# A two-layer hybrid decoder trunk on one core: reordered projection groups, stepwise waits, first loads on one queue

## The chip, the cores and the metric

The kernel runs on one core of one Trainium2 chip. The metric is the device time of one execution in microseconds (us); lower is better. The kernel before took 1836.92 us in the median of three runs (1834.95 to 1837.13). The profile shows one execution in which every engine's instructions are recorded: TensorE (PE, with its weight loads as PEld), VectorE (DVE), ScalarE (ACT), GpSimd (POOL) and SyncE (SP), which issues nearly all DMA transfers.

## The reference

Sequence 512, model width 1024, two layers, all in float32. Each layer computes

```
h    = RMSNorm(x)
proj = h @ w_in                        # q_a, kv_a, g_a, q_b, k_b, v_b, uv
o_a  = sparse attention(q_a, kv_a, sigmoid(g_a))
         # 8 heads in 2 groups; per head: softmax over compressed blocks (keys and values
         # by a small gelu MLP), over selected blocks, over a window; gated sum of the three
o_b  = differential attention(q_b, k_b, v_b)
         # 4 heads: softmax(q1 k1) - lambda * softmax(q2 k2), times v, RMSNorm per head
o_c  = u * (causal W_s per 128-position chunk @ RMSNorm(gelu(v)) + b)   # SGU
x    = x + (sum over a, b, c of sigmoid(h @ w_merge + b) * (o @ w_branch)) @ w_out
h    = RMSNorm(x)
x    = x + (silu(h @ w1) * (h @ w3)) @ w2
```

and a last RMSNorm follows. Queries and keys of the attentions (but for the compressed branch) are rotated by position (RoPE). With 512 positions and 8 blocks of 64, all eligible blocks are selected, so the selected branch is a causal softmax over the whole sequence, as the window branch is.

## The kernel before

**Arithmetic.** The activations lie with channels on the partitions (tiles of 128 x 512). Each float32 operand is split into a high and a low part (`h`, `lo`), and each product is three matmuls of 512 columns (`mm3`, lines 172 to 174): high by high, low weights by high, high weights by low. Weights come in chunks of 128 x 1024 from DRAM (`wr`, 3 buffers), are split by a ScalarE copy (line 152) and a DVE or POOL subtraction (line 155) into `wh` and `wl` (3 buffers each). A chunk feeds 24 matmuls.

**Tasks and lanes.** `layer_tasks` lists the main work of a layer: tasks of dense matmuls, each with its weight chunks, taken in order by `run`. `kvc` and `u0` to `u3` are projections; `wk`, `wv` the compression MLPs; `vv` the v half of the SGU; `V` the sparse attention's values and gates; `KR`, `QA0`, `QA1`, `KB0`, `QB0`, `KB1`, `QB1` are groups of keys or queries with rotation, two chunks and 48 matmuls each; `vb` holds the values of the differential attention, four chunks; `merge_tasks` gives eight gates and eight branch products per branch; then come the output projection and the FFN. Beside the main work run two lanes (`aux_tasks`): one with the tables of sines and cosines, the compression tails (`cmpk`, `cmpv`) and the SGU, one with the attention: `nsa0`, `nsa1` (query groups of the sparse attention, each 32 units of one head, branch and 128-row block) and `diff0`, `diff1`. Every `yield` of a main task is worth its planned nanoseconds (650 for three matmuls of 512 columns), and the lanes step until they have spent as much; a lane's step is worth what it yields (W_NSA, W_DIFF or a number). A task or lane entry starts only when all in its `need` list is done; a main task that needs a lane's work makes the lanes step without main work beside them.

**Ticks.** `later(n, f)` puts f off by n ticks; a tick is one main or lane step. `ensure(key)` runs at once all that is put off under the key, `settle(key, w)` yields w until none is left. D_ROPE holds the ticks between a rotated group's evacuation and its high copy, its low part, its write to DRAM and its read back; D_OA those of the head outputs.

**Order on the engines.** The program's text gives each instruction its priority; a list scheduler of the framework then sets each engine's order from estimated durations, so an instruction can be passed by a later one that is estimated to be ready sooner. All engines and SP work their queues in order.

**Rotation.** `rope_pair` (lines 613 to 673) multiplies the two PSUM results by cosine and sine on DVE, combines them on POOL (lines 633, 634), splits on ScalarE and DVE (638, 641), writes eight pieces `rp_d` to DRAM (line 649) and reads them back with another layout (`q` in four reads, line 669; keys in eight, line 661).

**Sparse attention.** `nsa` computes per unit the logits (lines 827, 828), a row minimum on DVE (816), an exponential on ScalarE (818), the scaling with the gate on POOL (853), a transpose on TensorE (870), its split on ScalarE (871) and DVE (877), and the product with the values into the one PSUM bank `o` (891). `cmp_soft` does the compressed branch, with a mask on POOL (776). A head's result lies in two halves of 64 partitions that have to be added: ScalarE copies the lower half to SBUF (`otmp`, line 907), and a tick later DVE adds the upper half from PSUM (910), once per head.

**Buffers.** Tiles of 4 KB per partition share 36 slots (`t4`), those of 2 KB 12 slots (`t2`).

**Start.** `setup` loads the first two weight chunks on ScalarE's queue, and on SP's the parameters, x in five transfers, a third chunk, x again by rows and the constants; TensorE meanwhile runs 12 matmuls on zeros.

Of the kernel before, what the change touches and what calls it, by code (L numbers as in the profile page):

```python
# [11 lines left out]
F32 = mybir.dt.float32  # L12
# [16 lines left out]

D_FIN = (10, 17, 31, 34)  # L30
D_CMP = (0, 5, 8, 12, 15, 26)
D_ROPE = (2, 11, 16, 19)
D_MX, D_ACT, D_OA, D_XP = (25, 27), (7, 19), (1, 4, 17), 2
D_NORM = (10, 13)
W_NSA, W_DIFF, LAG = 500, 1300, 3
WARM = 12
POOLED = {"g": 512}
(P_AN, P_FN, P_BM, P_SG, P_SUB, P_PK, P_PV, P_FIN) = (0, 8, 16, 40, 44, 45, 61, 77)
# [39 lines left out]
class Kern:  # L78
# [11 lines left out]


    def t4(self, name, shape, dt=F32):
        return self.sb.tile(shape, dt, name=name, tag="t4", bufs=36)

    def t2(self, name, shape=(P, S), dt=F32):
        return self.sb.tile(list(shape), dt, name=name, tag="t2", bufs=12)

    def small(self, name, n, bufs=4):
        return self.sb.tile([P, n], F32, name=name, tag=name, bufs=bufs)
# [122 lines left out]
    def setup(self):  # L222
# [3 lines left out]
        wh = [self.sb.tile([P, 1024], F32R, name="wh", tag="wh", bufs=3) for _ in range(2)]  # L226
        wl = [self.sb.tile([P, 1024], F32R, name="wl", tag="wl", bufs=3) for _ in range(2)]
        warm = self.t2("warm", dt=BF16)
        for j in range(2):
            nc.scalar.dma_start(raw[j], A["wst"][self.index(j)[0]])  # L230
        nc.sync.dma_start(self.par[0], A["par"][0])
        for k in range(2):
            nc.sync.dma_start(self.xT[0][:, k, :], A["xT"][0, :, k, :])
        for c in range(1, 4):
            nc.sync.dma_start(self.xT[c], A["xT"][c])
        self.ones = self.const("ones", [P, 2])
        nc.gpsimd.memset(self.ones, 1.0)
        self.mhalf = self.const("mhalf", [P, 4])
# [4 lines left out]
        wp = self.bank("t")  # L243
        for _ in range(WARM):
            nc.tensor.matmul(wp, warm[:, 0:P], warm, start=True, stop=True)
        half = [slice(0, S), slice(S, 2 * S)]
        self.n_dma = 2
        tok = [self.t4("xtok", [P, 1024]) for _ in range(TT)]
        self.dma_to(2)
# [361 lines left out]
    def rope_pair(self, name, raw=None):  # L611
# [13 lines left out]
        def fb(ps):  # L625
            nc = self.nc
            t2, t3 = self.t2("t2"), self.t2("t3")
            if raw is not None:
                nc.scalar.activation(st["raw"][:, 1, :], ps, AF.Copy)
            nc.vector.tensor_tensor(t2, ps, self.sinR, op=OP.mult)  # L630
            nc.vector.tensor_tensor(t3, ps, self.cosR, op=OP.mult)
            o1, o2 = st["t1"], st["t4"]
            nc.gpsimd.tensor_tensor(o1, o1, t2, op=OP.subtract)
            nc.gpsimd.tensor_tensor(o2, o2, t3, op=OP.add)
            pcs = [self.t4("pc", [P, 2, S], F32R) for _ in range(2)]
            for p, o in zip(pcs, (o1, o2)):
                def hi(p=p, o=o):
                    nc.scalar.activation(p[:, 0, :], o, AF.Copy)

                def lo(p=p, o=o):  # L640
                    nc.vector.tensor_tensor(p[:, 1, :], o, p[:, 0, :].bitcast(F32), op=OP.subtract)
                self.later(D_ROPE[0], hi, name)
                self.later(D_ROPE[1], lo, name)

            def out():
                d = self.dr.tile([4, 32, 4, S], F32, name="rp_d", tag="rp_d", bufs=2)
                for j, p in enumerate(pcs):
                    for h in range(4):
                        nc.sync.dma_start(d[j::2, :, h, :].rearrange("a p t -> p a t"),
                                          p[32 * h:32 * h + 32].bitcast(F32))  # L650
                st["d"] = d

            def back():
                d = st["d"].rearrange("a p h t -> (a p) h t")
                if name[0] == "K":
                    kh = [self.t4("kh", [P, 2, S], F32R) for _ in range(2)]
                    kl = [self.t4("kl", [P, 2, S], F32R) for _ in range(2)]
                    for c in range(2):
                        for x, k in enumerate((kh, kl)):
                            for r in range(2):  # L660
                                nc.sync.dma_start(k[c][64 * r:64 * r + 64].bitcast(F32),
                                                  d[64 * x:64 * x + 64, 2 * c:2 * c + 2, :])
                    self.rot[name] = (kh, kl)
                else:
                    q = [self.t4("q2", [P, 2, S], F32R) for _ in range(2)]
                    for c in range(2):
                        for j in range(2):
                            h = 2 * c + j
                            nc.sync.dma_start(q[c][:, j, :].bitcast(F32), d[:, h, :])
                    self.rot[name] = q  # L670
            self.later(D_ROPE[2], out, name)
            self.later(D_ROPE[3], back, name)
# [158 lines left out]
    def nsa(self, g):  # L831
# [47 lines left out]
        def sC(u):  # L879
# [21 lines left out]
            if half == 1 and kind == 1:  # L901
                ob = OB.pop(hh).rearrange("p a t -> p (a t)")
                if hh % 2 == 0:
                    st["o"] = self.t2("oa")
                oo = st["o"]
                tmp = self.t2("otmp")
                nc.scalar.activation(tmp[0:64], ob[64:128], AF.Copy)

                def fin():
                    nc.vector.tensor_tensor(oo[64 * (hh % 2):64 * (hh % 2) + 64], ob[0:64], tmp[0:64], op=OP.add)  # L910
                self.later(D_OA[0], fin, "oa")
                if hh % 2 == 1:
                    t = self.t4("oa", [P, 2, S], F32R)
                    self.oa[2 * g + hh // 2] = t

                    def hi_():
                        nc.scalar.activation(t[:, 0, :], oo, AF.Copy)

                    def lo_():
                        nc.vector.tensor_tensor(t[:, 1, :], oo, t[:, 0, :].bitcast(F32), op=OP.subtract)  # L920
                    self.later(D_OA[1], hi_, "oa")
                    self.later(D_OA[2], lo_, "oa")
# [316 lines left out]
    def layer_tasks(self, l):  # L1239
# [85 lines left out]
        g_w("k", 3)  # L1325
        g_vv(2)
        g_vv(3)
        g_w("v", 0)
        add("V", [("v", c) for c in range(3)], g_v)
        g_w("v", 1)  # L1330
        add("KR", [("KR", "A"), ("KR", "B")], g_kr, need=["tables"])
        g_w("v", 2)
        g_w("v", 3)
        add("QA0", [("QA0", "A"), ("QA0", "B")], g_rope("QA0", 0))
        add("QA1", [("QA1", "A"), ("QA1", "B")], g_rope("QA1", 1))
        self.merge_tasks(add, l, "c", True, False, ["sgu"])
        add("vb", [("vb", c) for c in range(4)], lambda i0: self.tm(i0, self.xg, self.vb_evac, 2, 512))
        add("KB0", [("KB0", "A"), ("KB0", "B")], g_rope("KB0"), need=["nsa1"])
        add("QB0", [("QB0", "A"), ("QB0", "B")], g_rope("QB0"))
        add("KB1", [("KB1", "A"), ("KB1", "B")], g_rope("KB1"))  # L1340
        add("QB1", [("QB1", "A"), ("QB1", "B")], g_rope("QB1"))
        self.merge_tasks(add, l, "a", False, False, ["nsa1"])
# [29 lines left out]
    def aux_tasks(self, l):  # L1372
# [9 lines left out]
        Y = []  # L1382

        def nsa(g):
            if g == 0:
                yield 7000
            self.ensure("QA%d" % g)
            self.cmp_soft(g)
            yield from self.nsa(g)

        def diff(p):
            if p == 0:
                yield 7000
            self.ensure("QB%d" % p)
            yield from self.diff(p)
        Y.append(("nsa0", ["V%d" % l, "QA0%d" % l, "cmpv%d" % l], lambda: nsa(0)))
        Y.append(("nsa1", ["QA1%d" % l], lambda: nsa(1)))
# [167 lines left out]
```

## Time and profile before

| | |
|---|---|
| median of three runs | 1836.92 us (1834.95 to 1837.13) |
| the profiled execution | 1836.91 us |
| its span | 1835.1 us, 23472 instructions |
| busy: PE, PEld, DVE, ACT, POOL | 1788.1, 1490.7, 979.4, 729.4, 372.0 us |
| chain that ended last, by engine | PE 88%, DVE 5%, POOL 2%, ACT 2%, issue 2%, DMA 1% |
| DMA | 208.45 MB, 114 GB/s in the mean |

Busy time is the time in which an engine executes an instruction; matmuls are pipelined and overlap, so a busy TensorE is not TensorE at its peak. The chain that ended last is followed back from the last instruction, at each step to what released it or to the instruction before it on its engine.

### The profile page before, as it was taken

Reading aid. Unit: us, or ns where it says so; the run is one execution under the profiler, and the core shown is the slowest. Engines: PE = TensorE matmul, PEld = TensorE weight load, DVE = VectorE, ACT = ScalarE, POOL = GpSimd, SP = SyncE. Lnnn points to the kernel's source line nnn. Section 1 sums busy time; section 2 is a strip of 40 time slices with the busy share of each in tenths; the row PEclk is TensorE's granted clock in tenths of the full one; section 3 lists DMA queues with packets and bytes.
Section 4 is the critical chain, followed back from the end, with each engine's and each line's share of the span. In section 5 each row is a group of like instructions: output and inputs, shape, how many; then the busy total and the mean of one; then the engine's idle time right before and its main releaser. Section 6 shows DMA issues by size and latency. Waiting matters only on the chain.

```text
span 1835.1 us, 23472 instructions
## 1 busy us (share of the span) xinstructions
PE 1788.1 (97%) x8690; PEld 1490.7 (81%) x8690; DVE 979.4 (53%) x1931; ACT 729.4 (40%) x1303; POOL 372.0 (20%) x363
## 2 busy tenths in 40 slices
PE   9998999999999999999999899999999999999997
PEld 6886888778888888888888778887788888888887
DVE  7766774656454444433357576656555544444323
ACT  5535663345343233222334366634443432332222
POOL 0124331344330000000012343314443200000001
PEclk9999999999999999999999999999999999999999
DMA  6472112743232222223243621145422322222221
GB/s 246 154 215 90 36 64 90 217 136 133 81 115 92 96 100 92 103 93 126 106 148 112 189 81 53 58 135 171 168 101 98 109 92 95 101 92 103 92 102 59
DMA packets 71441, 208.45 MB, mean 114 GB/s; under 512 B 9376, under 2 KB 11808, under 8 KB 71328
## 3 DMA queue, kind: packets, MB, share of 16 engines
q1 hardware_dynamic: 71040, 205.91, 33.8%
q8 instruction: 69, 1.13, 0.2%
q10 hardware_dynamic: 288, 1.05, 0.2%
q14 instruction: 44, 0.36, 0.1%
HBM read 187.92 MB, written 19.01 MB: 113 GB/s over the span
## 4 chain that ended last, share of the span: by engine, by line
PE 88%; DVE 5%; POOL 2%; ACT 2%; issue 2%; DMA 1%; SPq 0%; DVEq 0%; POOLq 0%; ACTq 0%
PE ps_g L173 24%; PE ps_g L172 24%; PE ps_g L174 24%; PE ps_t L870 2%; PE ps_o L891 2%; PE ps_g L212 1%; PE ps_g L213 1%; PE ps_g L214 1%; PE ps_s L827 1%; PE ps_s L828 1%; DVE wl L155 1%; POOL mix L1072 1%; PE ps_o L988 1%; DVE e L816 1%; PE ps_o L212 1%
## 5 line engine op out<-in xcount | busy, mean ns | idle before, releaser
L152 ACT ACTIVATE wh<-wr 128x1024 fp32r<-128x1024 f32 (+2 forms) x320 | 315.6, 989 | 673.9 <-PE ps_g L174 372.9
L172 PE MATMUL ps_g<-xg,wh 128*128 128x512 f32 x1400 | 553.8, 396 | 4.0 <-DVE sm L961 1.6
L173 PE MATMUL ps_g<-xg,wl 128*128 128x512 f32 x1400 | 548.3, 392 | 2.2 <-DVE wl L155 2.2
L174 PE MATMUL ps_g<-xg,wh 128*128 128x512 f32 x1400 | 547.2, 391 | 0.0
L155 DVE TENSOR_TENSOR wl<-wr,wh 128x1024 fp32r<-128x1024 f32 (+2 forms) x308 | 359.3, 1169 | 256.2 <-ACT wh L152 255.2
L172 PEld LDWEIGHTS ps_g<-xg,wh 128*128 128x128 f32 x1400 | 263.7, 188 | 57.3 <-ACT e L818 1.9
L174 PEld LDWEIGHTS ps_g<-xg,wh 128*128 128x128 f32 x1400 | 263.7, 188 | 55.3
L173 PEld LDWEIGHTS ps_g<-xg,wl 128*128 128x128 f32 x1400 | 264.3, 189 | 53.4 <-DVE wl L155 3.3
L818 ACT ACTIVATE e<-e,nm 128x128 f32<-128x128 f32 (+1 forms) x192 | 107.1, 559 | 118.9 <-DVE nm L816 112.6
L172 PE MATMUL ps_g<-act,wh 128*128 128x512 f32 (+1 forms) x374 | 141.0, 377 | 0.0
L173 PE MATMUL ps_g<-act,wl 128*128 128x512 f32 (+1 forms) x374 | 140.8, 376 | 0.0
L174 PE MATMUL ps_g<-act,wh 128*128 128x512 f32 (+1 forms) x374 | 140.8, 376 | 0.0
L853 POOL TENSOR_SCALAR e<-e,sm,ga 128x128 f32<-128x128 f32 (+3 forms) x128 | 82.9, 650 | 144.0 <-DVE sm L852 126.2
L816 DVE CUSTOM_DVE_ANT_0 e<-ps_s,con 128x128 f32<-128x128 f32 (+1 forms) x192 | 91.5, 482 | 33.1 <-PE ps_s L828 31.3
L452 POOL TENSOR_TENSOR acc<-acc,sq 128x512 f32<-128x512 f32 x18 | 29.4, 1634 | 381.1 <-ACT sq L451 381.1
L1129 DVE TENSOR_TENSOR fb<-ps_g,R 128x512 f32<-128x512 f32 x44 | 30.4, 692 | 129.1 <-PE ps_g L174 129.1
L155 POOL TENSOR_TENSOR wl<-wr,wh 128x512 fp32r<-128x512 f32 x48 | 71.9, 1497 | 99.3 <-ACT wh L152 67.9
L1120 DVE TENSOR_TENSOR fa<-ps_g,R 128x512 f32<-128x512 f32 x44 | 30.4, 692 | 95.3 <-PE ps_g L174 95.3
L173 PEld LDWEIGHTS ps_g<-act,wl 128*128 128x128 f32 x374 | 70.4, 188 | 13.0
L172 PEld LDWEIGHTS ps_g<-act,wh 128*128 128x128 f32 x374 | 70.4, 188 | 12.8
L174 PEld LDWEIGHTS ps_g<-act,wh 128*128 128x128 f32 x374 | 70.4, 188 | 12.8
L877 DVE TENSOR_TENSOR pt<-ps_t,pt 128x128 fp32r<-128x128 f32 (+3 forms) x128 | 61.4, 487 | 22.8 <-ACT pt L871 21.2
(242 smaller groups left out, 2574.3 us busy)
## 6 DMA issues: line engine op xcount, KB each, us to landing
wr<-in_wst SPq DMA_DIRECT2D x266, 512.0 KB, 3.2
rp_d<-pc SPq DMA_DIRECT2D x112, 128.0 KB, 2.5
wr<-in_wst SPq DMA_DIRECT2D x48, 256.0 KB, 2.8
q<-rp_d SPq DMA_DIRECT2D x32, 256.0 KB, 3.9
kh<-rp_d SPq DMA_DIRECT2D x24, 256.0 KB, 6.0
kl<-rp_d SPq DMA_DIRECT2D x24, 256.0 KB, 7.1
xT<-in_xT SPq DMA_DIRECT2D x7, 512.0 KB, 6.8
xtok<-in_xtok SPq DMA_DIRECT2D x4, 512.0 KB, 9.0
```

What stands on the lines that cost most here:

```text
L152: nc.scalar.activation(h[:, :w], t[:, :w], AF.Copy)
L155: eng.tensor_tensor(lo[:, a:b], t[:, a:b], h[:, a:b].bitcast(F32), op=OP.subtract)
L172: nc.tensor.matmul(out, wh[:, c], xx[:, 0, ts], start=first, stop=False)
L173: nc.tensor.matmul(out, wl[:, c], xx[:, 0, ts], start=False, stop=False)
L174: nc.tensor.matmul(out, wh[:, c], xx[:, 1, ts], start=False, stop=last)
L212: nc.tensor.matmul(o, x[k][:, 0, ts], wh[:, sl], start=(k == 0), stop=False)
L816: nc.vector.tensor_tensor_reduce(out=e[:, :n], in0=s[:, :n], in1=self.mask[:, S - n:], scale=-0.125, scalar=3e38, op0=OP.add, op1=OP.min, ...
L818: nc.scalar.activation(e[:, :n], e[:, :n], AF.Exp, bias=nm, scale=-1.0, accum_out=sm)
L853: nc.gpsimd.tensor_scalar(e[:, :n], e[:, :n], sm, gate, op0=OP.mult, op1=OP.mult)
L870: nc.tensor.transpose(pt[:, j, :], e[:, j * P:(j + 1) * P], self.ident)
L877: nc.vector.tensor_tensor(lo, pt, hi.bitcast(F32), op=OP.subtract)
L891: nc.tensor.matmul(o[:, c0:], self.V2[kind][:, j, g, :], t[:, j, c0:], start=(kind == 0 and j == 0 and x == 0), stop=False)
```

## The change

- `setup`: ScalarE's queue loads only the parameters. SP's queue brings x and the first two weight chunks by turns, in pieces of 128 x 512 for the first four: x tile 0, first half of chunk 0, x tile 1, first half of chunk 1, x tiles 2 and 3, second half of chunk 0, x tiles 4 and 5, second half of chunk 1, x tiles 6 and 7.
- Order of main tasks: KR comes directly behind the last `vv`, QA0 between `wv1` and `wv2`, V behind `wv3`. `vb` moves from before KB0 to behind QB0.
- D_ROPE goes from (2, 11, 16, 19) to (2, 6, 9, 14), W_DIFF from 1300 to 1250; a query group is read back in two transfers in place of four.
- Lanes: `nsa0` and `diff0` no longer yield 7000 first; all four attention entries call `settle` and not `ensure` for their queries.
- Head outputs: ScalarE copies both halves of a head out of PSUM, into the rows of a tile for two heads; one DVE addition over 128 partitions follows per two heads.
- Slots: `t4` 35 for 36, `t2` 14 for 12.

```diff
-D_ROPE = (2, 11, 16, 19)
+D_ROPE = (2, 6, 9, 14)
-W_NSA, W_DIFF, LAG = 500, 1300, 3
+W_NSA, W_DIFF, LAG = 500, 1250, 3
-        return self.sb.tile(shape, dt, name=name, tag="t4", bufs=36)
+        return self.sb.tile(shape, dt, name=name, tag="t4", bufs=35)
-        return self.sb.tile(list(shape), dt, name=name, tag="t2", bufs=12)
+        return self.sb.tile(list(shape), dt, name=name, tag="t2", bufs=14)
...
-        for j in range(2):
-            nc.scalar.dma_start(raw[j], A["wst"][self.index(j)[0]])
-        nc.sync.dma_start(self.par[0], A["par"][0])
-        for k in range(2):
-            nc.sync.dma_start(self.xT[0][:, k, :], A["xT"][0, :, k, :])
+        half = [slice(0, S), slice(S, 2 * S)]
+
+        def load_w(j, k):
+            nc.sync.dma_start(raw[j][:, half[k]], A["wst"][self.index(j)[0], :, half[k]])
+        nc.scalar.dma_start(self.par[0], A["par"][0])
+        nc.sync.dma_start(self.xT[0][:, 0, :], A["xT"][0, :, 0, :])
+        load_w(0, 0)
+        nc.sync.dma_start(self.xT[0][:, 1, :], A["xT"][0, :, 1, :])
+        load_w(1, 0)
         for c in range(1, 4):
             nc.sync.dma_start(self.xT[c], A["xT"][c])
+            if c < 3:
+                load_w(c - 1, 1)
...
-                        for j in range(2):
-                            h = 2 * c + j
-                            nc.sync.dma_start(q[c][:, j, :].bitcast(F32), d[:, h, :])
+                        nc.sync.dma_start(q[c].bitcast(F32), d[:, 2 * c:2 * c + 2, :])
...
                 if hh % 2 == 0:
-                    st["o"] = self.t2("oa")
-                oo = st["o"]
-                tmp = self.t2("otmp")
-                nc.scalar.activation(tmp[0:64], ob[64:128], AF.Copy)
-
-                def fin():
-                    nc.vector.tensor_tensor(oo[64 * (hh % 2):64 * (hh % 2) + 64], ob[0:64], tmp[0:64], op=OP.add)
-                self.later(D_OA[0], fin, "oa")
+                    st["o"], st["lo"] = self.t2("oa"), self.t2("otmp")
+                oo, ol = st["o"], st["lo"]
+                rows = slice(64 * (hh % 2), 64 * (hh % 2) + 64)
+                nc.scalar.activation(oo[rows], ob[0:64], AF.Copy)
+                nc.scalar.activation(ol[rows], ob[64:128], AF.Copy)
                 if hh % 2 == 1:
+                    def fin():
+                        nc.vector.tensor_tensor(oo, oo, ol, op=OP.add)
+                    self.later(D_OA[0], fin, "oa")
...
         g_vv(2)
         g_vv(3)
+        add("KR", [("KR", "A"), ("KR", "B")], g_kr, need=["tables"])
         g_w("v", 0)
-        add("V", [("v", c) for c in range(3)], g_v)
         g_w("v", 1)
-        add("KR", [("KR", "A"), ("KR", "B")], g_kr, need=["tables"])
+        add("QA0", [("QA0", "A"), ("QA0", "B")], g_rope("QA0", 0))
         g_w("v", 2)
         g_w("v", 3)
-        add("QA0", [("QA0", "A"), ("QA0", "B")], g_rope("QA0", 0))
+        add("V", [("v", c) for c in range(3)], g_v)
         add("QA1", [("QA1", "A"), ("QA1", "B")], g_rope("QA1", 1))
         self.merge_tasks(add, l, "c", True, False, ["sgu"])
-        add("vb", [("vb", c) for c in range(4)], lambda i0: self.tm(i0, self.xg, self.vb_evac, 2, 512))
         add("KB0", [("KB0", "A"), ("KB0", "B")], g_rope("KB0"), need=["nsa1"])
         add("QB0", [("QB0", "A"), ("QB0", "B")], g_rope("QB0"))
+        add("vb", [("vb", c) for c in range(4)], lambda i0: self.tm(i0, self.xg, self.vb_evac, 2, 512))
         add("KB1", [("KB1", "A"), ("KB1", "B")], g_rope("KB1"))
...
         def nsa(g):
-            if g == 0:
-                yield 7000
-            self.ensure("QA%d" % g)
+            yield from self.settle("QA%d" % g, W_NSA)
             self.cmp_soft(g)
             yield from self.nsa(g)

         def diff(p):
-            if p == 0:
-                yield 7000
-            self.ensure("QB%d" % p)
+            yield from self.settle("QB%d" % p, W_NSA)
             yield from self.diff(p)
```

## Rows read from the trace of the kernel before

**Rows 1.** The page: busy us, share of the span, instructions.
```profile
PE 1788.1 (97%) x8690; PEld 1490.7 (81%) x8690; DVE 979.4 (53%) x1931; ACT 729.4 (40%) x1303; POOL 372.0 (20%) x363
```

**Rows 2.** Windows: stretch, length, busy us (count) by engine, clock, DMA.
```profile
140.00:200.00 60.00, 50.83 (x290) 42.12 (x289) 42.46 (x140) 36.50 (x101) 27.06 (x37) 0.94 0.20 64
220.00:240.00 20.00, 18.73 (x110) 15.42 (x109) 15.81 (x56) 13.14 (x36) 9.70 (x13) 1.00 0.13 43
340.00:400.00 60.00, 55.23 (x276) 44.58 (x275) 36.30 (x102) 25.79 (x59) 27.59 (x21) 1.00 0.60 177
600.00:660.00 60.00, 60.00 (x266) 49.69 (x265) 28.32 (x34) 18.07 (x22) 0.00 (x0) 1.00 0.28 97
1040.00:1100.00 60.00, 51.30 (x280) 42.48 (x279) 39.52 (x131) 35.94 (x94) 27.61 (x36) 0.91 0.26 83
1240.00:1300.00 60.00, 55.31 (x264) 44.41 (x263) 33.40 (x98) 24.05 (x56) 24.70 (x19) 0.97 0.63 191
```

**Rows 3.** TensorE's waits, 138 to 200: releaser, us, times, longest.
```profile
PE ps_t L870 <- POOL e L853: 4.3, 1, 4.3
...
PE ps_o L891 <- DVE oa L910: 1.4, 1, 1.4
```

**Rows 4.** Timeline of POOL, 142 to 147: start us, us, instruction.
```profile
142.01 1.70 POOL L776 TENSOR_TENSOR ce<-ce,con 128x128 f32<-128x128 f32 x4 [3.73 <-DVE ce L771]
...
145.11 1.76 POOL L633 TENSOR_TENSOR t<-t,t 128x512 f32<-128x512 f32 x1 [1.40 <-DVE sm L852]
```

**Rows 5.** Timeline, 117 to 133: the rotation of QA0.
```profile
117.84 0.69 DVE L630 TENSOR_TENSOR t<-ps_g,sinR 128x512 f32<-128x512 f32 x1 [1.47 <-ACT raw L629]
...
119.86 2.27 POOL L634 TENSOR_TENSOR t<-t,t 128x512 f32<-128x512 f32 x1
...
125.96 1.28 DVE L641 TENSOR_TENSOR pc<-t,pc 128x512 fp32r<-128x512 f32 x2
...
126.67 3.80 SPq L649 DMA_DIRECT2D rp_d<-pc  x8
...
131.01 1.80 SPq L669 DMA_DIRECT2D q<-rp_d  x4
```

**Rows 6.** The page's DMA issues: count, KB each, us to landing.
```profile
rp_d<-pc SPq DMA_DIRECT2D x112, 128.0 KB, 2.5
...
q<-rp_d SPq DMA_DIRECT2D x32, 256.0 KB, 3.9
```

**Rows 7.** TensorE's waits, 340 to 400.
```profile
PE ps_s L827 <- DMA q<-rp_d: 1.6, 2, 1.3
...
PE ps_t L1017 <- DVE do L1012: 0.9, 1, 0.9
```

**Rows 8.** Groups by line: the steps that empty a head's bank.
```profile
L907 ACT ACTIVATE otmp<-ps_o 64x512 f32<-64x512 f32 x16 | 9.5, 596 | 8.6 <-PE ps_o L897 8.1
...
L910 DVE TENSOR_TENSOR oa<-ps_o,otmp 64x512 f32<-64x512 f32 x16 | 10.9, 684 | 11.9 <-ACT otmp L907 11.9
```

**Rows 9.** Timeline, 131 to 137: a subtraction on POOL, and DVE.
```profile
131.10 1.28 POOL L155 TENSOR_TENSOR wl<-wr,wh 128x512 fp32r<-128x512 f32 x1 [8.97 <-ACT wh L152]
...
136.44 0.69 DVE L155 TENSOR_TENSOR wl<-wr,wh 128x512 fp32r<-128x512 f32 x1 [8.00 <-ACT wh L152]
...
136.49 1.79 POOL L155 TENSOR_TENSOR wl<-wr,wh 128x512 fp32r<-128x512 f32 x1 [4.10 <-ACT wh L152]
```

**Rows 10.** Timeline of the start: first tile, first matmuls.
```profile
6.74 0.48 DVE L274 TENSOR_SCALAR xg<-xT,par 128x512 fp32r<-128x512 f32 x1 [5.62 <-DMA xT<-in_xT]
...
7.37 0.47 PE L172 MATMUL ps_g<-xg,wh 128*128 128x512 f32 x1 [0.90 <-DVE xg L274]
...
9.16 0.50 PE L172 MATMUL ps_g<-xg,wh 128*128 128x512 f32 x1 [1.31 <-ACT wh L269]
```

**Rows 11.** SP's wait before rotary writes; the chain at 1286.
```profile
SPq L649 <- DVE pc L641: 70.9, 10, 15.4
...
1286.01 4.99 DMA wr<-in_wst
```

More of the change, by code (lines that the diff above doesn't have):

```diff
@@ L245, in setup @@
             nc.tensor.matmul(wp, warm[:, 0:P], warm, start=True, stop=True)
-        half = [slice(0, S), slice(S, 2 * S)]
         self.n_dma = 2
```

## The prediction

> **What bounds the kernel now.** I read the busy times first: TensorE is busy 1788 of 1835.1 us [rows 1], so a change can only win what TensorE loses. Then I cut the span into 20 us windows, to see where. Nearly all of the loss stands in a few places that come once per layer; [rows 2] sums them over 60 us each. A dense stretch (600 to 660) holds 266 matmuls of 512 columns, 0.2256 us each, and no idle time. Against it:
> - [...] Layer 2, 1040 to 1100: 8.7 + 0.09 x 60 = 14.1.
> - 340 to 400 (first pair of the differential attention starts): 4.8. Layer 2, 1240 to 1300: 4.7 + 0.03 x 60 = 6.5.
>
> These add up to 38.2 us. Some half-clock time falls on idle time, so it is a little less; on the other side the idle column misses that matmuls behind a wait start further apart.
>
> The waits of TensorE, and then the timeline, say why. Shortly before 148 TensorE waits 4.3 us for the POOL step that scales the first softmax rows (`e`) [rows 3]. POOL was busy with the mask of the compressed branch (1.70 us from 142.01) and with a rotary product of group QA1 (1.76 us from 145.11) [rows 4]. All of this comes late and at once, because the attention could not begin: QA0 left TensorE before 117.84, when its last products begin on DVE, but its rotated halves are split on DVE at 125.96, written to DRAM from 126.67, read back from 131.01 [rows 5], and such a read lands 3.9 us after its issue [rows 6]: about 136.4. The round trip is thus 18.5 us. Meanwhile TensorE ran ahead through QA1 and the first merge gates; when the attention came, the work that should have lain beside it was used up. The differential attention has the same pattern: it waits for `q` from DRAM (1.6 us) and then for `do` (0.9) [rows 7].
>
> **The change, part by part.** The sum starts from the profiled execution, 1836.9 us, which is the median of the three runs as well.
>
> *Order of the groups, and the first query group.* QA0 now stands in front of wv2, wv3 and V. These give the round trip cover: V has 96 matmuls of 280 columns, by the dense rate 96 x 0.2256 x 280/512 = 11.8 us; wv2 and wv3 have 8 each of 256 columns, 0.9 us each: 13.6 us. The round trip gets shorter too: D_ROPE puts the low half 6 instead of 11 ticks behind the evacuation, the write 9 instead of 16, the read 14 instead of 19. From [rows 5], POOL was done at 122.13 and the split on DVE ended only at 127.24; done at once, a ScalarE copy (0.6 us, as the one in [rows 8]) and the two 0.64 us splits would end near 124. The eight writes need 3.8 us of SP, partly beside the splits, and about 2.5 us to land [rows 6]; two reads in place of four save 0.9 us of issue. That gives some 15 us, against 13.6 of cover: `q` is 1 to 2 us late (4.9 if nothing gets shorter), and QA1 (48 matmuls, 10.8 us) lies beside it. `yield 7000` goes, so the attention starts with QA1 and not 11 of its 16 steps later. Then the start should look like that of the second query group, whose `q` is long there: 1.3 us idle in 220 to 240 [rows 2]. I leave 1.3 + 1.7 = 3 us per layer. Bounds: 0, and all of 12.8 and 14.1. Gain 9.8 + 11.1 = 20.9.
>
> *vb behind QB0.* vb is 96 matmuls of 512 columns, 21.7 us, more than the measured round trip of 18.5. The 1.6 us wait for `q` and the crowding around it go; `do` (0.9) and some 0.6 of first waits stay: 1.5 us per layer. Gain 3.3 + 5.0 = 8.3; bounds 0 and 11.3. W_DIFF at 1250 makes the two pairs 12 x 3 x 1250 x 2 = 90,000 ns of planned steps, and from KB1 to the fourth gate of merge B there are 160 x 650 = 104,000: enough, so nothing is forced there.
>
> *What the move takes away.* KB0 needs the second query group finished. That group and the first have 37 x 2 x 500 x 2 = 74,000 ns of planned steps, and from QA1 to the end of merge C there are 16 x 650 + 8 x 12 x 650 = 72,800. vb used to absorb the rest; now about three steps are forced ahead of KB0. They are the drained end of the pipeline. I price them at 0.5 us per layer, 1.0 in all (0 to 1.2 us each, the missing steps). SGU now stands beside KR and QA0 rather than V; its two short waits move with it: 0, plus or minus 1.
>
> *Head outputs.* Today a head's result leaves PSUM by a ScalarE copy of 0.60 us and then a DVE add of 0.68 us; the one bank is held until the add ends, and TensorE waited 1.4 us for it once per layer [rows 3, 8]. Now two ScalarE copies free it, 1.2 us by the same row: the same duration, without DVE's queue in between. The 1.4 us is inside the 12.8 already, so nothing is added. ScalarE takes 16 x 0.6 = 9.6 us more over the run, beside TensorE; bounds -1 to +1 us per layer. The add now has both inputs in SBUF, over 128 partitions, once per two heads (8 times). [rows 9] show what that can do: POOL's subtraction of a 128x512 tile took 1.28 us, and 1.79 when a DVE subtraction with two SBUF inputs ran beside it: +0.51. So 8 x 0.51 = 4 us of POOL time at most; POOL has over half of its time free there [rows 2] and a scaled row is used three units later. I take 0, and keep 4 as the upper bound.
>
> [...]
>
> *First loads.* Before, TensorE began its first real matmul at 7.37, when DVE had made the first tile from the load at 6.74, and its second at 9.16, waiting 1.31 us for a weight split [rows 10]. In between, 1 MB of weights on ScalarE's queue and x on SP's share the engines. By need, 0.25 MB of x and 0.25 MB of weights come first, so the first matmul can follow the last warm-up (7.37 - 0.90 = 6.47). The two idle stretches are the upper bound, 0.9 + 1.3 = 2.2 us; the lower is 0, since the bytes ahead of the last tile of x stay the same, and DVE's chain of splits follows it. I take two thirds: 1.5.
>
> *Buffers.* One 4 KB slot fewer, two 2 KB slots more: 0, unless a slot is missing (in the range).
>
> Sum: 20.9 + 8.3 + 1.5 - 1.0 = 29.7; 1836.9 - 29.7 = 1807.2 us.
>
> **Rivals.**
> *A. The first query group stays half exposed.* If the round trip keeps its 18.5 us, 4.9 us stick out of the 13.6; DVE works its queue in order and sits on the first softmax step, with weight splits behind it. Half of the 20.9 is lost: 1818. For it: three weight chunks share SP with the writes. Against: QA1 is still there as cover.
>
> *B. Order unchanged.* The order on each engine comes from estimated times, not from the text alone: in the trace QA1 and two gates overtook the attention. If this happens at both starts again, only the 1.5 us of the first loads less the 1.0 stays: 1836. Against: at the second group's start, with its data there, it did not.
>
> *C. SP's single queue starves TensorE: slower.* SP stood 70.9 us in total, 15.4 at the longest, in front of a rotary write waiting for its split, and weight loads stand behind it; at 1286 such a load, issued late, took 4.99 us on the chain of waits, just ahead of the half clock of [rows 2, 11]. Writes and reads are now issued 7 and 5 ticks earlier, so they can wait longer at the head of SP. It decides where SP's wait outlasts the weights already loaded. Priced at 2.5 us for each of the 14 rotary groups, 35 us go and 29.7 come: 1842. Against: the splits come 5 ticks earlier as well, so what SP waits for is also sooner.
>
> *D. All goes.* Nothing left at both starts: 38.2 + 2.2 off, 1796, and down to 1788 if matmuls behind waits also close up, by a fifth more.
>
> **How the numbers follow.** Forecast 0.58 (own range 1797 to 1817), A 0.14, B 0.08, C 0.12, D 0.08. No change means within 0.2%, or 3.7 us, about what a measurement of this kernel can tell. Faster: forecast, A and D, 0.80; same: B, 0.08; slower: C, 0.12. The range 1788 to 1836 takes in D, A and most of B, and leaves out C.
>
> **What would show it.** In the changed trace: first logits near the start of QA1; the longest wait for `e` under 1.5 us, and no half clock near the two starts; no wait of TensorE for `q` at the start of the differential attention; first real matmul near 6.5; POOL's `e` no longer than now. It is wrong if the idle time of the 60 us around each start stays above 7 us, or if TensorE waits on weight splits behind late loads (C).

## The result, and the profile after

The changed kernel took 1822.46 us (median of 4 runs, 1821.77 to 1823.33) against 1836.36 us for the kernel before beside it: ratio 0.9925 [0.9908, 0.9943]. That is 13.9 us of the 29.7 us forecast: the direction was right, and the size less than half. The profiled execution took 1821.8 us, its span is 1820.0 us, 15.1 us less than before: TensorE's busy time fell by 10.1 us, its idle time by 5.0.

The page's busy row, after (columns as in [rows 1]):

```profile
PE 1778.0 (98%) x8690; PEld 1487.4 (82%) x8690; DVE 981.7 (54%) x1923; ACT 743.2 (41%) x1319; POOL 376.5 (21%) x363
```

TensorE's row of the windows of the kernel after (stretch, length, busy us (count), clock, DMA share, GB/s), for the stretches that answer to [rows 2]:

```profile
80.00:100.00 20.00, 19.05 (x102) 1.00 0.44 141
100.00:120.00 20.00, 16.66 (x105) 0.83 0.83 233
120.00:140.00 20.00, 18.94 (x112) 1.00 0.44 158
140.00:160.00 20.00, 17.30 (x97) 0.91 0.34 107
160.00:220.00 60.00, 58.06 (x348) 1.00 0.15 53
340.00:400.00 60.00, 58.08 (x297) 1.00 0.52 153
980.00:1000.00 20.00, 19.05 (x102) 1.00 0.53 165
1000.00:1020.00 20.00, 17.63 (x134) 1.00 0.82 246
1020.00:1040.00 20.00, 15.76 (x71) 0.91 0.35 120
1040.00:1060.00 20.00, 17.34 (x106) 1.00 0.36 107
1060.00:1120.00 60.00, 58.05 (x348) 1.00 0.15 53
1240.00:1300.00 60.00, 58.08 (x297) 1.00 0.49 144
```

The start of the sparse attention now lies across more windows, so for a fair sum the neighbours of [rows 2] in the kernel before are needed too (same columns; those not shown lose nothing):

```profile
100.00:120.00 20.00, 19.33 (x96) 1.00 0.71 209
...
980.00:1000.00 20.00, 19.45 (x141) 1.00 0.38 133
1000.00:1040.00 40.00, 39.33 (x192) 1.00 0.71 212
...
1120.00:1140.00 20.00, 18.73 (x109) 1.00 0.16 52
```

Counted as the prediction counted, idle time plus the part lost at the half clock (a granted share of 0.50, as from 110.8 to 117.5 after):

| | before | after | gained | forecast |
|---|---|---|---|---|
| sparse start, layer 1 | 0.7 + 12.8 + 1.3 = 14.8 | 1.0 + 6.7 + 1.1 + 4.5 + 1.9 = 15.2 | -0.4 | 9.8 |
| sparse start, layer 2 | 0.6 + 0.7 + 14.1 + 1.3 = 16.7 | 1.0 + 2.4 + 6.0 + 2.7 + 1.9 = 14.0 | 2.7 | 11.1 |
| differential start, layer 1 | 4.8 | 1.9 | 2.9 | 3.3 |
| differential start, layer 2 | 6.5 | 1.9 | 4.6 | 5.0 |

These columns show 9.8 of the 15.1 us. They miss that matmuls behind waits start further apart: in 340 to 400 TensorE now does 297 matmuls where it did 276 [rows 2], though only 2.9 us less are idle. So the differential start gave what was forecast, and the sparse start of layer 1 gave nothing. The loss there didn't stay where it was: it moved to other places. These are TensorE's longest waits in 80 to 160 (two), in 1000 to 1030 and in 340 to 400 (operation, releaser, us, times, longest):

```profile
PE ps_t L873 <- DVE sm L855: 2.5, 1, 2.5
PE ps_g L212 <- ACT wh L152: 2.3, 1, 2.3
...
PE ps_g L172 <- ACT ga L687: 3.9, 1, 3.9
PE ps_g L212 <- ACT wh L152: 1.2, 1, 1.2
...
PE ps_s L830 <- DVE nm L819: 1.9, 1, 1.9
```

ScalarE ahead of the 3.9 us wait, and DVE ahead of the 2.5 us wait, from the timelines:

```profile
1023.34 1.06 ACT L152 ACTIVATE wh<-wr 128x1024 fp32r<-128x1024 f32 x1 [3.62 <-DMA wr<-in_wst]
1024.30 0.61 ACT L687 ACTIVATE ga<-ps_g,r4h 128x24 f32<-128x24 f32 x3
```

```profile
149.47 1.08 DVE L646 TENSOR_TENSOR pc<-t,pc 128x512 fp32r<-128x512 f32 x1 [2.30 <-ACT pc L643]
```

The 4.3 us wait for POOL's `e` and the 1.4 us wait for the head's bank [rows 3] are gone, and the waits for `q` and `do` of [rows 7] as well. In their place TensorE waits for V's weights (line 212), in layer 2 for a bank that ScalarE empties late (line 687), behind the split of a chunk that landed late (1023.34), and at the differential start for a row minimum. The wait of 2.5 us near 149 comes in both layers (in layer 1 with half clock behind it, 0.50 from 151.7 to 155.0; 4.5 us lost in 140 to 160): DVE stands 2.30 us for a half of QA1 before it splits it, and the reciprocal of a softmax sum (`sm`, line 855) comes only behind that split, at 150.94.

**Why V's weights are late, and `q` with them.** SP's own rows in the timeline of the changed kernel (start us, us, instruction) show one queue with two kinds of transfers:

```profile
101.38 1.24 SPq L666 DMA_DIRECT2D kl<-rp_d  x2
102.71 1.71 SPq L135 DMA_DIRECT2D wr<-in_wst  x3
108.41 0.33 SPq L654 DMA_DIRECT2D rp_d<-pc  x1
113.62 0.33 SPq L135 DMA_DIRECT2D wr<-in_wst  x1
114.00 3.59 SPq L654 DMA_DIRECT2D rp_d<-pc  x7
119.36 0.34 SPq L672 DMA_DIRECT2D q<-rp_d  x1
```

And the other engines between them (at the end of a row: idle before it, and releaser):

```profile
104.47 0.68 DVE L635 TENSOR_TENSOR t<-ps_g,sinR 128x512 f32<-128x512 f32 x1
...
107.28 1.94 DVE L646 TENSOR_TENSOR pc<-t,pc 128x512 fp32r<-128x512 f32 x2 [1.22 <-ACT pc L643]
...
111.62 1.46 ACT L152 ACTIVATE wh<-wr 128x840 fp32r<-128x840 f32 x2 [3.12 <-DMA wr<-in_wst]
...
112.56 1.69 DVE L155 TENSOR_TENSOR wl<-wr,wh 128x840 fp32r<-128x840 f32 x2 [2.54 <-ACT wh L152]
...
124.87 0.31 PE L830 MATMUL ps_s<-kh,q 128*128 128x128 f32 x1
```

Read it in both directions. The loads of V's last two chunks and of QA1's first stand behind KR's eight reads and go from 102.71; V's land 8.8 us after their issue, with the reads beside them (the load at 113.62 lands after 3.9), and ScalarE stands 3.12 us for them. And QA0's two halves are split at 109.2 (107.28 + 1.94), but after one write the seven others go only at 114.00: in front of them stands a weight load that waits for a buffer, which comes free when DVE has split V's late chunk (112.56). The eight writes thus take 9.2 us (108.41 to 117.59). The two reads go at 119.36 and 120.34 and land 4.1 and 5.7 us later. From the last products (104.47) it is 19.0 us to the first half of `q` and 21.6 to the second; by the same count it was 17.5 and 18.8 in the kernel before. The first logits (124.87) don't wait for `q`: they stand behind V, which is late itself. The next weight chunk, the first gate's, is held as well: its load goes at 119.75, behind the writes and the first read of `q`; in layer 2 it is this chunk that is split at 1023.34, ahead of the 3.9 us wait.

### The profile page after: what moved, and what is told of

Its sections match the earlier page's. It is cut to its first block, busy times and chain, and to the rows that moved or that the text cites. A ratio compares the mean times of both kernels' runs of the same rounds, so it can differ in the third digit from the quotient of the medians.

```text
span 1820.0 us, 23429 instructions
## 1 busy us (share of the span) xinstructions
PE 1778.0 (98%) x8690; PEld 1487.4 (82%) x8690; DVE 981.7 (54%) x1923; ACT 743.2 (41%) x1319; POOL 376.5 (21%) x363
## 4 chain that ended last, share of the span: by engine, by line
PE 87%; DVE 5%; DMA 2%; POOL 2%; ACT 2%; issue 1%; SPq 0%; DVEq 0%; ACTq 0%; POOLq 0%
PE ps_g L172 24%; PE ps_g L174 24%; PE ps_g L173 24%; PE ps_o L894 2%; DMA wr<-in_wst 2%; PE ps_t L873 2%; PE ps_g L212 1%; PE ps_s L831 1%; PE ps_g L213 1%; PE ps_g L214 1%; PE ps_s L830 1%; PE ps_o L991 1%; POOL mix L1075 1%; DVE wl L155 1%; ACT wh L152 1%
## 5 line engine op out<-in xcount | busy, mean ns | idle before, releaser
L152 ACT ACTIVATE wh<-wr 128x1024 fp32r<-128x1024 f32 (+1 forms) x320 | 315.6, 989 | 670.2 <-PE ps_g L174 343.1
L155 DVE TENSOR_TENSOR wl<-wr,wh 128x1024 fp32r<-128x1024 f32 (+2 forms) x308 | 355.3, 1156 | 227.2 <-ACT wh L152 226.2
L172 PEld LDWEIGHTS ps_g<-act,wh 128*128 128x128 f32 x374 | 70.4, 188 | 12.8
```

Of the source, the lines that this page charges most:

```text
L152: nc.scalar.activation(h[:, :w], t[:, :w], AF.Copy)
L155: eng.tensor_tensor(lo[:, a:b], t[:, a:b], h[:, a:b].bitcast(F32), op=OP.subtract)
L172: nc.tensor.matmul(out, wh[:, c], xx[:, 0, ts], start=first, stop=False)
```

## The experiments

All ratios are to the kernel before on the same chip, five rounds each. Where a kernel is "the changed kernel with ...", it is to be set against 1822.5 us (0.9925).

**The parts alone.** First `vb` behind QB0, in the kernel before:

```diff
-        add("vb", ...)          # ahead of KB0
+        add("vb", ...)          # behind QB0
 def diff(p):
-    if p == 0:
-        yield 7000
-    self.ensure("QB%d" % p)
+    yield from self.settle("QB%d" % p, W_NSA)
```

> Only vb behind QB0 and settle in the two entries of the differential attention, all else as before (ticks 2, 11, 16, 19, W_DIFF 1300). Theory (this move gave nearly the whole gain; losses of TensorE around the start of the differential attention fell by 12 us in the two layers together): 1836.4 - 12 = 1824 us, within 3. Rival (the gain there needs the shorter ticks, or came from the first group's new place): 1830 or more.

Measured: 1828.65, ratio 0.9955 [0.9943, 0.9968], 7.8 us less, between the two expectations. The term was forecast at 8.3.

Then the order KR, QA0, V with `settle` in `nsa`, in the kernel before, with the old ticks:

> Only the order KR, wv0, wv1, QA0, wv2, wv3, V and settle in the two entries of the sparse attention; old ticks, old vb. Theory (the late q is replaced by late weights of V and QA1, which share SP and the DMA engines with the rotary traffic of KR and QA0): 1831 to 1838 us, no more than 5 gained, and TensorE or ScalarE waits for weight loads within V. Rival (the order is good and the shorter ticks spoil it): 1826 or less, no such wait.

Measured: 1831.46, 0.9969 [0.9957, 0.9980], 5.0 us less. The time is the theory's, the cause only in part: of TensorE's waits there `q` is the largest (V's low parts, line 213, cost 2.8 us):

```profile
PE ps_s L827 <- DMA q<-rp_d: 10.7, 4, 3.8
```

The changed kernel with the old ticks, `D_ROPE = (2, 11, 16, 19)`:

> The changed kernel with the rotation's ticks of before (2, 11, 16, 19). Theory (late weights come from the traffic itself, whatever the ticks): 1822 within 3 us, ScalarE still waits for V's weights. Rival (shorter ticks put rotary steps at the head of ScalarE, DVE and SP): 1812 to 1816.

Measured: 1831.17, 0.9976 [0.9967, 0.9985]. Both expectations missed: without the shorter ticks 8.7 us of the 13.9 are lost, `q` is late again (a wait of 4.9 us), and the parts don't add up: with the old ticks they came to 7.8 + 5.0 alone, and to 5.3 together with the rest.

The changed kernel with the first loads of before:

> The changed kernel with the first loads of before. Theory (TensorE's loss in the first 40 us is 7.7 us against 7.9, so the new order of loads gives nothing): 1822 to 1823 us. Rival (the first loads give what the prediction said): 1824 us or more.

Measured: 1821.21, 0.9915 [0.9901, 0.9928]: the first loads by need give nothing. And with the old way out for the head outputs:

> The changed kernel with the old way out for the head outputs: one ScalarE copy and one DVE add from PSUM per head. The prediction took this part at nothing (minus 2 to plus 6 us for the whole kernel): 1820.5 to 1824.5. [...] Other rival (it holds the PSUM bank less, and that was a good part of the gain): over 1825.

Measured: 1823.38, 0.9931 [0.9918, 0.9943], the same as the changed kernel within the uncertainty, as forecast.

**Taking the wait for V's weights away.** Four kernels, each with one edit in the changed kernel. Keys read back in four transfers of 128 partitions in place of eight of 64:

```diff
-    for r in range(2):
-        nc.sync.dma_start(k[c][64 * r:64 * r + 64].bitcast(F32),
-                          d[64 * x:64 * x + 64, 2 * c:2 * c + 2, :])
+    v = d[64 * x:64 * x + 64, 2 * c:2 * c + 2, :]
+    two = bass.AP(tensor=v.tensor, offset=v.offset, ap=[[0, 2]] + [list(a) for a in v.ap])
+    nc.sync.dma_start(k[c].bitcast(F32), two)
```

> The changed kernel (1822.5), but a rotated key group is read back in four DMAs of 128 partitions (256 KB each, the source repeated) in place of eight of 64. Theory (what took the place of the late q is SP's single queue: V's weights stand behind the eight writes and eight reads of KR, and are split 2 to 3 us late, which also brings the half clock from 110.7 to 117.5): four issues fewer bring V's first chunk some 2.5 us sooner; the wait of 2.3 us and most of the 3.4 us at half clock go, in layer 1 above all: 1816 to 1819. Rival (the DMA engines are full at 97 to 119, the bytes decide, and these are the same): 1821 to 1824, with V's weights as late as before.

Measured: 1986.72, 1.0816 [1.0802, 1.0831], 164 us slower than the changed kernel; neither theory had this. SP's rows and the windows of this kernel:

```profile
98.58 7.20 SPq L667 DMA_DIRECT2D kh<-rp_d  x1
105.83 9.87 SPq L667 DMA_DIRECT2D kl<-rp_d  x1
```

```profile
110.00:120.00 10.00, 0.00 (x0) 0.51 0.13 52
```

The DMA engines are busy at 0.13, as much as two of sixteen, and move 52 GB/s; an issue on SP takes 7 to 10 us there, where two of the changed kernel's took 1.24 (101.38), and TensorE does nothing. The source's outer dimension is the repeat of 2; that this is the reason isn't shown. With reads this slow the run says nothing on the number of issues, and its theory wasn't tested by it.

wv0 to wv2 spread between the `vv` chunks:

> The changed kernel, but wv0 to wv2 (256-column matmuls, each chunk of 512 KB feeds only 0.9 us of TensorE) stand between the vv chunks, and only wv3 between KR and QA0, so that the weights of wv2, wv3 and V no longer come in one burst behind KR's rotation. Theory (burst of weights behind the rotation on SP): the loss at 100 to 120 of layer 1 (6.9 us) goes down to 2, but QA0 stands nearer to V and its q has 0.9 us less cover: 1815 to 1819. Rival (the burst is not it; TensorE loses to whatever is next in the rotation): 1821 to 1825.

Measured: 1821.66, 0.9919 [0.9906, 0.9932], no change. Four buffers for weight chunks (`bufs=4` for `wr`, 34 slots of `t4`):

> The changed kernel with four landing buffers for weight chunks in place of three (and 34 slots of 4 KB in place of 35): a load may be issued one chunk, 0.9 to 5.4 us, sooner. Theory (V's and QA1's weights come late because their loads are issued late): both waits for a split behind a late load (2.3 us near 112, 3.9 us near 1024) and the half clock after them go: 1813 to 1818. Rival (the loads stand behind the rotation's reads and the engines are full, so an earlier request only moves the queue): 1820 to 1824; a missing 4 KB slot would make it slower than 1824.

Measured: 1824.59, 0.9937 [0.9925, 0.9950], no gain either. KR's reads behind V's weight loads:

```diff
-            self.later(D_ROPE[3], back, name)
+            self.later(D_ROPE[3] + (16 if name == "KR" else 0), back, name)
```

> The changed kernel, but KR's rotated keys are read back 16 ticks later, so that on SP's queue V's three weight loads and the next one stand in front of these eight reads and not behind them. Theory (V's weights are late because they stand behind KR's reads in one queue): TensorE's wait for V's first split (2.3 us near 112) goes, and the half clock at 110.7 to 117.5 with it; QA0's q is then uncovered for 1 to 2 us, as the prediction had it: net 1817 to 1821. Rival (the DMA engines are simply full, order doesn't matter): 1821 to 1824, V's split as late. Rival (q or the keys are late instead, by as much): 1821 to 1825, with TensorE waiting for q or k near 130 in place of the split.

Measured: 1830.27, 0.9968 [0.9956, 0.9981]. In these three the wait for V's high part (line 212) is gone, and others have its place, above all one for `q` (with the spread also 3.4 us for V's low parts). TensorE's rows for `q`, in turn (the changed kernel's is 0.2 us):

```profile
PE ps_s L830 <- DMA q<-rp_d: 4.3, 2, 2.5
```

```profile
PE ps_s L830 <- DMA q<-rp_d: 3.0, 3, 1.7
```

```profile
PE ps_s L830 <- DMA q<-rp_d: 11.4, 2, 5.9
```

So V's late weights had hidden that `q` is late too. The last rival of the third run, which said this, held as to the wait (its time came out some 5 us longer still).

**More cover.** QA1 in front of V, `W_NSA = 425`; and the same with wv0 to wv2 spread:

> The changed kernel with QA1 moved in front of V (order KR, wv0, wv1, QA0, wv2, wv3, QA1, V) and 425 ns planned for a step of the sparse attention in place of 500, since QA1's 16 steps no longer lie beside it. Theory (the first query group lacks dense work between QA0's evacuation and the first use of q, and QA1's own rotation stands in the queues of ACT and DVE at the first softmax): q gets 10.8 us more cover, V's weights are due 10.8 us later, QA1's rotation drains beside V; of the some 18 us lost in 80 to 160 of layer 1 and 1000 to 1060 of layer 2 each, two thirds of what hangs on these waits (V's or QA1's weights, q, the transposes for sm) go, some 6 us per layer: 1808 to 1813. Rival (any new group starts with the same loss wherever it stands, because DVE, ACT and POOL fill their pipelines in order): 1819 to 1825.

> Both: QA1 in front of V with 425 ns a step, and wv0 to wv2 spread between the vv chunks. If the two causes (burst of weights, too little cover) are separate, the gains add: 1806 to 1811. If the spread only moved its loss onto q, and QA1's cover takes that away as well, this is where the spread shows its own gain against the version without it: 2 to 3 us. Rival (the spread costs at the wv chunks themselves, 5 us near 40 to 80): as the version without it or up to 3 us slower.

Measured: 1830.43, 0.9972 [0.9961, 0.9983], and 1825.96, 0.9949 [0.9935, 0.9962]: both slower than the changed kernel. Two of TensorE's waits in the first one:

```profile
PE ps_s L830 <- DVE nm L819: 15.1, 12, 1.9
PE ps_g L172 <- ACT ga L687: 4.7, 2, 2.4
```

The waits for V's evacuation (`ga`) are about those of the changed kernel (4.4 us), but those for row minima were 4.1 us there, in four. The softmax begins right behind V, whose products end at 134.9; ScalarE copies V's banks only at 144.43, between softmax steps, so the dense gates can't start, and TensorE has nothing to do beside the logits. That QA1 between V and the attention gives the evacuation its time is argued from this; as `W_NSA` was changed with it, the two aren't told apart. The gain that the theory forecast (too little dense work) didn't come.

**The queue itself.** QA0's rotary writes on ScalarE's queue, the rest as in the changed kernel:

```diff
-    nc.sync.dma_start(d[j::2, :, h, :]...
+    (nc.scalar if name == "QA0" else nc.sync).dma_start(d[j::2, :, h, :]...
```

> The changed kernel, but the eight rotary writes of QA0 are issued on ScalarE's queue and not on SP's. In the changed kernel's trace QA0's halves are split at 109.2, one write goes at 108.4, and the other seven stand from there to 114.0 behind a weight load that waits for its buffer. Theory (one queue couples the weight loads and the rotation, and both directions cost): q lands some 4 us earlier, but V's weights, behind KR's reads, stay 2 to 3 us late and bound alone: 1819 to 1822. If q was what really held the first softmax: 1814 to 1818. Rival (the queue isn't the cause; ScalarE pays 8 x 0.45 us of issue and its waits): 1822 to 1827.

Measured: 1815.32 (1814.35 to 1818.26), 0.9889 [0.9875, 0.9902]: 7.1 us less than the changed kernel, with intervals that don't overlap, and the fastest kernel here; the time is that of the second case, not of the theory. Its rows on SP, ScalarE and TensorE:

```profile
102.44 10.69 SPq L135 DMA_DIRECT2D wr<-in_wst  x5
...
108.32 1.79 ACTq L654 DMA_DIRECT2D rp_d<-pc  x2
...
110.50 1.56 PE L768 MATMUL ps_t<-KAB,raw 128*128 128x128 f32 x12
...
111.26 3.42 ACTq L654 DMA_DIRECT2D rp_d<-pc  x6
...
122.62 0.44 PE L830 MATMUL ps_s<-kh,q 128*128 128x128 f32 x1 [2.37 <-DMA q<-rp_d]
```

The writes are out at 114.7 and not at 117.6, and the first logits come 2.2 us earlier; they now wait 2.37 us for `q`, and half clock follows. The first gate's load no longer stands behind writes and reads: it goes at 112.81 and not at 119.75, in layer 2 at 1009.82 and not at 1016.68, and the 3.9 us wait of layer 2 is gone. The waits for V's weights (3.5 us in the two layers) are down to 0.2, and the half clock near 112 is gone, but not because the loads go earlier: they still stand behind KR's reads (102.44; 102.71 in the changed kernel), and in layer 2 V's second chunk is split 8.7 us after its load's issue, against 7.5. In layer 1 TensorE's order is another: the transposes of the raw queries (`raw`, 110.50) now stand ahead of V's second chunk. The waits for `sm` fall too, from 4.9 us to:

```profile
PE ps_t L873 <- DVE sm L855: 1.6, 2, 0.8
```

The windows with the gain and the loss in layer 1:

```profile
100.00:120.00 20.00, 18.95 (x144) 1.00 0.88 260
120.00:140.00 20.00, 17.20 (x79) 0.91 0.37 129
```

So the edit is worth 7.1 us, but how much of that is the queue and how much the new order on the engines that came with it isn't shown.

More of the same is no better. KR's reads on ScalarE's queue as well, and the late reads of KR with QA0's writes there:

> As the kernel with QA0's writes on ScalarE's queue, and KR's eight reads there too, so that SP has V's weight loads right behind KR's writes. Theory (one queue): both V's weights and q come in time, the two losses near 100 to 130 and 1000 to 1030 (some 9 us per layer, of which the transposes at 148 are no part) go down by half or more: 1811 to 1816. Rival (the DMA engines are full there, so the order of issue only moves the loss): 1820 to 1824. Rival (ScalarE, in order, stands for KR's writes to land and holds QA0's PSUM banks): slower than 1824.

> As the kernel with KR's reads 16 ticks later (1830.3, where q is 5.9 us late in both layers), but with QA0's writes on ScalarE's queue. Theory (q is late there because its writes stand behind KR's reads and a weight load on SP): most of the 11.4 us of waits for q go: 1817 to 1822. Rival (q is late through its splits or its reads, or the engines are full): 1827 to 1831.

Measured: 1826.78, 0.9945 [0.9933, 0.9958], and 1822.49, 0.9927 [0.9914, 0.9941]. The second is 7.8 us below the same kernel with the writes on SP (1830.27), so the edit is worth much the same there. The first has the second rival's time and effect (ScalarE holds QA0's banks), but not its cause: KR's writes are issued by 96.4 and land 2.4 to 2.8 us later, before the reads begin. It is issuing the eight reads that takes ScalarE from 101.54 to 107.17; QA0's first bank is copied only then, and not at 102.19. Its rows:

```profile
101.54 1.14 ACTq L666 DMA_DIRECT2D kh<-rp_d  x2
...
105.81 1.36 ACTq L666 DMA_DIRECT2D kl<-rp_d  x2
107.22 0.60 ACT L625 ACTIVATE raw<-ps_g 128x512 f32<-128x512 f32 x1 [4.93 <-DMA kl<-rp_d]
```

Last, all groups' writes there, QA0's writes there in the kernel before, and QA0's writes there with the old first loads:

> The changed kernel with the rotary writes of all seven groups per layer on ScalarE's queue. Theory (only where weight loads are scarce, behind QA0, do they hold a rotary write back; elsewhere the dense work covers the round trip): as with QA0's alone, 1814 to 1817, or a little more where ScalarE waits for a split: up to 1820. Rival (the coupling costs at all fourteen groups): 1806 to 1812.

> The kernel before, with QA0's rotary writes on ScalarE's queue and nothing else changed. Theory (there, q was late because the halves were split late, on DVE at 125.96, 11 ticks behind; SP wrote at 126.67 at once, so its queue was no part): 1834 to 1837.5, no gain. Rival (SP's queue held q back in the kernel before as well): 1825 to 1831.

> The changed kernel with QA0's rotary writes on ScalarE's queue (1815.3) and with the first loads of the kernel before (1821.2 in place of 1822.5 when done alone, within the uncertainty). If the two are independent: 1813.5 to 1816, at or below the better of the two. If the old first loads shift the order on the engines into another of the arrangements seen above: over 1817.

Measured: 1820.14, 0.9904 [0.9889, 0.9919]; 1833.89, 0.9984 [0.9975, 0.9993]; 1817.76, 0.9895 [0.9881, 0.9910]. With all groups' writes there the kernel is no faster than with QA0's alone. That doesn't say that the queue costs nothing elsewhere: at the differential start no loss is left (58.08 us busy in the changed kernel),

```profile
340.00:400.00 60.00, 60.00 (x307) 1.00 0.53 154
```

but at the sparse start more is lost (in 120 to 140 TensorE is busy 14.99 us at 0.83): KR's writes leave later by ScalarE, V's loads go at 106.07 and not at 102.44, and TensorE waits 4.7 us for `q` in layer 1. In the kernel before, QA0's writes alone are worth 2.9 us (between the two expectations), in the changed one 7.1, with KR's late reads 7.8, and with the old first loads 3.4 (1821.21 to 1817.76, intervals that overlap). The direction is the same in all four; the size hangs on what else is in the kernel. The old first loads add nothing on top.

## Why the prediction was right or wrong

**The step that failed** is the length of the first query group's round trip: "The eight writes need 3.8 us of SP, partly beside the splits", "That gives some 15 us, against 13.6 of cover". The splits did come early: 4.7 us behind the last products began (104.47 to 109.2), where the prediction's "near 124" is 6.2. The writes took 9.2 us in place of 3.8, as a weight load waiting for its buffer stood among them, and the trip took 19.0 us to the first half of `q` and 21.6 to the second. I had costed SP by the instructions that it issues, and not by what they wait for in order. The prediction's own sign of being wrong came: TensorE waited on weight splits behind late loads (2.3 and 1.2 us).

**The cover** was sized by TensorE's time alone (11.8 us for V). But V's three chunks, wv2 and wv3 bring 2144 KB in 13.6 us of planned matmuls, just behind KR's rotation; in 100 to 120 the DMA engines are busy at 0.83. The matmuls that were to hide the trip waited for the same queue, and so `q` was no longer seen to be late: a wait of 0.2 us that looks solved. QA1 was counted as cover too, but its own rotation stands on DVE in front of the first softmax steps (2.5 us per layer, with half clock behind it in layer 1). The "1.3 + 1.7 = 3 us per layer" became 15.2 and 14.0 over the wider stretch, where 14.8 and 16.7 were lost before. The 12.8 us that the forecast's 9.8 starts from are 9.2 us idle and 0.06 x 60 = 3.6 at the half clock [rows 2]; no run shows this clock as a frequency, only as a share: 0.50 from 146.5 to 153.3 in the kernel before.

**Was `q` what held the start?** In the kernel before, `q` had landed by 136.7 and the first logits ran at 140.59, in layer 2 by 1043.4 and at 1045.31: at the sparse starts TensorE didn't wait for `q` at all. The trip that the prediction set out to shorten ended 3.9 and 1.9 us before the logits; what released these isn't shown.

**The outcome is nearest to rival A's in size (1818, 4.5 us below the measured time), with the mechanism of rival C in part.** C was right that SP's queue couples rotation and weights. I had only looked at one direction, a write waiting for its split [rows 11]. SP's wait in front of rotary writes went down from 70.9 us; SP's own row after is

```profile
SPq L654 <- DVE pc L646: 49.7, 14, 12.9
```

What the rows show beside it is the other direction: writes behind a waiting weight load, and a weight load behind writes and reads that wait. With QA0's writes off SP 7.1 us come back, of the 15.8 that the forecast missed; the rest isn't traced to one cause. C's price of 2.5 us at each of 14 groups was too high: with all groups' writes off SP the kernel is no faster than with QA0's alone.

**vb behind QB0** (8.3): 7.8 alone, 7.5 in the windows. The reason given holds: 21.7 us of dense work cover the trip, and the wait for `q` of [rows 7] is gone. vb's four chunks come by the same queue, 2048 KB, about as many bytes as behind QA0, but in 21.7 us and not in 13.6.

**First loads** (1.5): nothing. TensorE's first real matmuls, after:

```profile
5.41 0.58 PE L172 MATMUL ps_g<-xg,wh 128*128 128x512 f32 x1
...
8.62 0.80 PE L172 MATMUL ps_g<-xg,wh 128*128 128x512 f32 x1 [2.63 <-ACT wh L274]
```

The first one comes 2 us sooner than in [rows 10], even sooner than forecast; the second only 0.5 us. In 4 to 6 us the DMA engines, as busy as before (0.99 and 1.03), move 159 GB/s where it was 372; that the smaller pieces are the reason isn't shown. The one idle stretch of 2.6 us is longer than the two of before together.

**Head outputs** (0): 0.9 us, within the uncertainty. The 1.4 us wait for the bank is gone, but with the old way out too, so that isn't this part's doing. ScalarE works 11.8 us more (743.2 against 731.4 with the old way). POOL works 376.5 against 373.8 us: 2.7 us more, below the 4 taken as the upper bound from [rows 9]; TensorE waits for POOL's `e` for 0.4 us in the whole run. None of the eight new additions on DVE (0.69 us each) has a POOL instruction beside it in the trace.

**The tail** (-1.0): nothing to be seen; 260 to 280, ahead of KB0, is dense, TensorE is busy 19.97 of 20 us.

**What stays open.** In the fastest kernel the same columns still give some 10 us per sparse start: `q` is late by 4.0 us over the two layers, with half clock behind it, and the rest is in shorter waits. Why QA0's writes and the old first loads together are no better than the writes alone wasn't settled, nor why the same edit is worth 2.9 us in one kernel and 7.8 in another.

## What to carry to other kernels

A queue that works in order is costed by its waits, in both directions: ask of each transfer what stands in front of it and what that one waits for. Ask of cover what it needs from the same queue in that time: 2048 KB in 21.7 us covered the trip, 2144 KB in 13.6 us did not. When a wait vanishes, take away the one that has taken its place and see whether the first comes back, before calling it solved. And when an edit moves instructions on several engines, look at their order before giving the whole gain to the queue.

## What the hardware showed beyond that

A read whose source repeats 64 rows by an outer dimension of 2 used as much as two of the sixteen DMA engines (share 0.13, 52 GB/s), and the kernel with 24 such reads was 164 us slower. QA0's eight writes took 5.2 us of issue on ScalarE in layer 1 and 3.7 in layer 2, in place of SP's, and the kernel was 7.1 us faster.
